# The down projection with seven products in every piece

## The chip, the cores and the metric

The kernel runs on one core of one Trainium2 chip. The metric is the time of one execution on the device in microseconds (us); smaller is better. All engines of the core work at once: TensorE (PE, with its weight loads as PEld), VectorE (DVE), ScalarE (ACT), GpSimd (POOL) and SyncE (SP). SP, ACT and POOL also issue DMAs, and each issues its own in the order of its queue.

## What is computed

One layer of a hybrid encoder on 512 tokens of width 2048, in float32. The part that matters here is the last one, the gated MLP with D_FF = 5504:

```
hn = rmsnorm(h, norm_ffn_g)
u = causal_dwconv(hn @ w_up, ffn_conv_w, ffn_conv_b)
gate, val = jnp.split(u, 2, axis=-1)
h = h + (jax.nn.silu(gate) * val) @ w_down
return rmsnorm(h, norm_out_g)
```

Before it come an mLSTM mixer and a short convolution (through `w_in`, `w_branch_m`, `w_branch_c`, `w_out`). The change touches the product with `w_down` (5504 x 2048) alone.

## The kernel before

**Products.** Every float32 operand is held as two rounded parts, hi and lo, and every product is three matmuls: hi by hi, hi by lo, lo by hi. Large products are made from pieces. A piece is a 2 x 2 block product: four blocks of weights (two output blocks, two pairs of the summed dimension) by blocks of activations of 256 tokens. By Strassen's scheme it takes 7 products, done for two halves r = 0, 1 of the summed dimension: 2 x 7 x 3 = 42 matmuls of 128 x 256. Done plainly it takes 8 products, 48 matmuls.

**A piece of seven products.** `weight_task` loads it into a `raw` buffer of seven slots (6 such buffers in all). A plain DMA on SP brings four blocks (L261). `fill` makes two sums while loading: SP copies a block into slots 4 and 5 (L251, L252), then POOL issues two DMAs that add a second block (L254). DVE makes the other two sums (L217, L222). ACT rounds each half to `wh` (L232, 4 buffers), DVE subtracts to get `wl` (L236, 3 buffers). **A piece of eight products** (`eight_task`) needs the four blocks alone: no L251, L252, L254, L217, L222; ACT has L185 and L186, DVE L190 and L191, twice each.

**Activations.** They are prepared two blocks at a time by a `cell_task`, which borrows a `raw` buffer as well. For seven products: the sums L343, L348, L353 on DVE, then 1792 columns in L357 (ACT) and L360 (DVE). For a pair that only pieces of eight products read: the difference L338, then 1536 columns in L357 and L360.

**Items.** An item is one pair of output blocks. Its pieces follow each other on PE; the first two items and the last two of a phase run piece by piece in turn. The down projection is three phases, here called chunks, of 8 items: chunk 1 has 4 pieces an item, chunks 2 and 3 have 3 (the last three blocks of the 5504 are done plainly at the end, in L1170 to L1172). Items are numbered 0 to 7 in a chunk. In the kernel before, the last piece of each item has eight products: 24 of the 80 pieces.

**After an item.** Six products gather in three PSUM banks of one of two sets, the seventh (P1) in bank 3, of which each set has one half. `evac_first` (L304, on ACT) copies P1 to a buffer `z`, and DVE adds the rest (L310 to L313). P1 of the next item is its first product in bank 3 and waits for that L304. There are three `z` buffers, used in turn, so item n + 3 takes the buffer of item n. The item's last act in the down projection is `down_post`: ACT changes a sign in `z` (L866), and POOL issues a DMA that adds `z` to `h_d` in DRAM (L156). L304 of item n + 3 has to wait until this DMA has landed.

**The order.** A loop over pieces (from L1303 on) writes the order of all engines by hand. In the turn of piece s it emits what DVE does for piece s + 1 (`wl`), the sums and `wh` for s + 2, cells that are due, the matmuls of s, `evac_first` if the item ends, and loads for as many buffers as are free by then. `down_post` is not tied to a turn. It waits in the list `posts` until a running account allows it:

```
                if not rush and cost and credit <= cost / 2 and len(x[1]) < due(x[0]) - s:
                    break
```

`credit` grows by 5.04 a piece and loses the costs that each task is given: 0.8 + 2.05 for a piece of seven, 0 + 1.5 for a piece of eight, 1.35 + 1.95 for a cell, 0.65 + 1.7 for a cell of eight, 2.3 for an evacuation. `due` is the last piece of item n + 3 in the down projection: one turn ahead of it, a post is let go whatever the account says. The order is fixed when the kernel is built.

Of the kernel before, what the change touches and what calls it, by code (L numbers as in the profile page):

```python
# [44 lines left out]
def kpair(c):  # L45

    q, r = divmod(c, 2)
    return 4 * q + r, 4 * q + 2 + r
# [23 lines left out]
def tile_block(ctx: ExitStack, tc: tile.TileContext, xT, w1, w_v0, w_v1, w_v2, w_bm, w_bc, w_out, w_up, w_down,  # L72
# [13 lines left out]
    def nm(s):  # L86
        uid[0] += 1
        return f"{s}_{uid[0]}"

    def f(ap):  # L90
        return ap.bitcast(F32)
# [4 lines left out]
    def slots(t):  # L96
        return t.rearrange("p (s n) -> p s n", n=SW)

    def two(ap):
        return ap.unsqueeze(1).to_broadcast([P, 2, ap.shape[-1]])  # L100
# [29 lines left out]
    def D_(shape, s):  # L130
        return dram.tile(shape, F32, name=s)
# [4 lines left out]
    a_d = D_([NF, P, T], "a_d")  # L136
# [16 lines left out]
    def add_to(dst, src, key):  # L153

        def fn():
            G.dma_start(dst, src, accum_op=ALU.add)  # L156
            stored.add(key)
        late.append(fn)

    def pair_ap(d, a, b):  # L160

        return d[a:b + 1:b - a].rearrange("j p t -> p j t")

    def sb_pair(t):
        return t[:, :2 * T].rearrange("p (j t) -> p j t", j=2)
# [79 lines left out]
    def fill(raw, srcs):  # L245

        def at(i):
            return raw[:, i * SW:(i + 1) * SW].rearrange("p (k n) -> p k n", n=P)

        a11, a12, a21, a22 = srcs  # L250
        SP.dma_start(at(4), a11)  # L251
        SP.dma_start(at(5), a22)  # L252
        for i in (4, 5):
            G.dma_start(at(i), a21, accum_op=ALU.add)  # L254

    def tiles_load(w, n1, n2, k0=0):
        def load(raw, q, bare=False):
            if not bare:
                fill(raw, [w[n, :, k0 + 4 * q + i:k0 + 4 * q + i + 2, :] for n in (n1, n2) for i in (0, 2)])
            src = w[n1:n2 + 1:n2 - n1, :, k0 + 4 * q:k0 + 4 * q + 4, :]  # L260
            SP.dma_start(raw[:, :4 * SW].rearrange("p (b m) -> p b m", b=2), src.rearrange("b p k n -> p b (k n)"))  # L261
        return load
# [53 lines left out]
    def cell_task(xs, c, d, scale=None, key=None, eight=False):  # L316

        k1, k2 = kpair(c) if isinstance(c, int) else c
        t = Task(None, None, None, None)

        def new_raw():
            t.raw = wp.tile([P, NW], F32, tag="raw", name=nm("xraw"), bufs=RAW)

        def load():
            new_raw()
            for dst, k in zip(t.two(), (k1, k2)):
                SP.dma_start(dst, d[k])

        def two_k():
            return (t.raw[:, :T], t.raw[:, T:2 * T]) if eight else (t.raw[:, 5 * SW:], t.raw[:, :2 * SW])  # L330

        def scaled():
            for ap, k in zip(two_k(), (k1, k2)):
                A.activation(ap, ap, AF.Copy, scale=scale(k))

        def diff():
            x = slots(t.raw)
            V.tensor_sub(x[:, 4:6], x[:, 0:4:2], x[:, 1:4:2])  # L338

        def t3():  # L340
            x = slots(t.raw)

            V.tensor_sub(x[:, 2:4], x[:, 1:6:4], two(x[:, 6]))  # L343

        def e():

            x = slots(t.raw)
            V.scalar_tensor_tensor(x[:, 4], x[:, 3], -1.0, x[:, 1], op0=ALU.mult, op1=ALU.subtract)  # L348

        def t4():  # L350

            x = slots(t.raw)
            V.scalar_tensor_tensor(x[:, 6], x[:, 4], -1.0, x[:, 0], op0=ALU.mult, op1=ALU.subtract)  # L353

        def hi():
            t.act = actp.tile([P, 2 * NW], F32R, tag="act", name=nm("act"))
            A.activation(t.act[:, :m], t.raw[:, :m], AF.Copy)  # L357

        def lo():
            V.tensor_sub(t.act[:, NW:NW + m], t.raw[:, :m], f(t.act[:, :m]))  # L360
            t.raw = None
            xs[t.cell] = t.act
            t.act = None

        t.load, t.sums, t.hi, t.lo, t.new_raw = load, [diff] if eight else [t3, e, t4], hi, lo, new_raw
        t.two, m = two_k, 6 * SW if eight else NW
        if scale:
            t.pre, t.behind = scaled, 1
        t.cost = (0.65, 1.7) if eight else (1.35, 1.95)
        t.ready = (lambda: all(k in stored for k in key)) if key else None  # L370
        return t
# [488 lines left out]
    def down_post(c, p):  # L860
        def post(it):
            j1, j2 = kpair(p)

            def fn():
                b = it.z[:, T:]
                A.activation(b, b, AF.Copy, scale=-1.0)  # L866
                add_to(pair_ap(h_d, j1, j2), sb_pair(it.z), ("d", c, p))
            return [(0.1, fn)]
        return post
# [24 lines left out]
    def phase(items, xs, cells, spread=(-4, -2, -1, 0, 2, 3, 5, 6)):  # L894

        inter = {0, len(items) - 2}
        e = len(steps)
        add(items, inter)
        for n, t in enumerate(cells):
            t.cell, t.xs, t.spread, t.after = n, xs, e + spread[n], 0  # L900
            if t.after_end:
                t.after_end.urgent = True
                t.after = [i for i in range(e) if steps[i][0] is t.after_end][-1] + 4
            use = [s for s in range(e, len(steps)) if steps[s][1] == n // 2]
            t.first, t.last = use[0], use[-1]
            all_cells.append(t)
# [86 lines left out]
    for c, (k0, nq) in enumerate(CHUNKS):  # L993
        AA = {}
        items = []
        for p in range(8):
            items.append(Item(tiles_load(w_down, *kpair(p), k0), nq, AA, down_post(c, p), None, nq - 1))
        cells = []
        for i in range(2 * nq):
            k1, k2 = (k0 + k for k in kpair(i))  # L1000
            cells.append(cell_task(AA, (k1, k2), a_d, None, [("a", k1), ("a", k2)], i >= 2 * nq - 2))
        phase(items, AA, cells)


# [237 lines left out]
    for i in range(at[START]):  # L1242
# [4 lines left out]
        while todo_mm:  # L1247
            s, r = todo_mm[0]
            it, q = steps[s]
            c = 2 * q + r  # L1250
# [245 lines left out]
```

## Time and profile before

| | |
|---|---|
| median of 3 runs | 2630.27 us (2627.07 to 2635.22) |
| profiled execution | 2635.24 us, its span 2633.5 us |
| PE busy, PEld busy | 2579.5 us, 2562.4 us |
| DVE, ACT, POOL busy | 2112.6, 1291.9, 799.5 us |
| matmuls | 21146, of them 20280 in L280 to L282 |
| mean granted TensorE clock | 0.990 |

The page is one execution: its span, and outside it 1.7 us. The tables by stretch give the microseconds that each engine was busy in a stretch and, in brackets, how many instructions it did. In rows of the timeline the first number is the start in us from the span's start, the second the time taken; idle time of the engine ahead of the row and what ended it stand in square brackets. On DVE an instruction's record overlaps that of the next a little, so what one costs in a row of others is the distance of the starts.

### The profile page before, as it was taken

The numbers are of one execution on the slowest core, as the hardware profiler recorded it, in microseconds if no ns is written. First come the engines' busy times: TensorE is split into PE (matmuls) and PEld (weight loads), VectorE is DVE, ScalarE is ACT, GpSimd is POOL, SyncE is SP. The second block draws the span as 40 slices with busy tenths as digits, with TensorE's granted clock in tenths as the row PEclk, the third lists the DMA queues.
The fourth block names the chain that finished last, engine by engine and source line by source line (L and its number), as shares of the span: only waits on it lengthen the run. The fifth ranks groups of instructions, "written<-read, shape, count | busy, mean of one in ns | idle before, by whom it ended". The sixth has DMA issues, their size and how long they took to land.

```text
span 2633.5 us, 55501 instructions
## 1 busy us (share of the span) xinstructions
PE 2579.5 (98%) x21146; PEld 2562.4 (97%) x21146; DVE 2112.6 (80%) x3308; ACT 1291.9 (49%) x1748; POOL 799.5 (30%) x922
## 2 busy tenths in 40 slices
PE   8999999999999999999899999999999999999997
PEld 8999999999999999999899999999999999999997
DVE  8577778886777888877989888888888897677756
ACT  7444554546556543435545544454444454444433
POOL 2443333333333211222333333333333323232310
PEclk8999999999999999999999999999999999999998
DMA  8799989898898897787898988988888889898976
GB/s 214 179 225 232 240 218 260 219 253 222 228 252 220 233 296 222 222 241 211 230 223 225 225 221 222 221 227 221 221 223 223 214 227 229 212 239 207 237 173 193
DMA packets 462557, 592.55 MB, mean 225 GB/s; under 512 B 42784, under 2 KB 296736, under 8 KB 462288
## 3 DMA queue, kind: packets, MB, share of 16 engines
q1 hardware_dynamic: 301968, 419.79, 50.8%
q0 software_dynamic: 133088, 124.04, 31.7%
q10 hardware_dynamic: 27232, 45.17, 4.7%
q8 instruction: 165, 2.70, 0.4%
q14 instruction: 104, 0.85, 0.1%
HBM read 531.17 MB, written 57.67 MB: 224 GB/s over the span
## 4 chain that ended last, share of the span: by engine, by line
PE 70%; DVE 4%; issue 1%; DMA 1%; ACT 0%; SPq 0%; DVEq 0%; POOL 0%; ACTq 0%; POOLq 0%
PE bank L282 22%; PE bank L280 22%; PE bank L281 22%; DVE wl L236 1%; DVE act L360 1%; DMA raw<-in_w_up_dram 1%; PE bank L1170 0%; PE bank L442 0%; PE bank L1171 0%; PE bank L1172 0%; PE bank L639 0%; DVE z L311 0%; DVE raw L217 0%; DVE z L310 0%; DVE xraw L343 0%
## 5 line engine op out<-in xcount | busy, mean ns | idle before, releaser
L280 PE MATMUL bank<-act,wh 128*128 128x256 f32 x6760 | 1929.3, 285 | 11.8 <-ACT wh L232 5.9
L282 PE MATMUL bank<-act,wl 128*128 128x256 f32 x6760 | 1920.5, 284 | 20.1 <-DVE wl L236 16.7
L281 PE MATMUL bank<-act,wh 128*128 128x256 f32 x6760 | 1917.9, 284 | 0.0
L282 PEld LDWEIGHTS bank<-act,wl 128*128 128x128 f32 x6760 | 1302.7, 193 | 24.0 <-DVE wl L236 19.9
L280 PEld LDWEIGHTS bank<-act,wh 128*128 128x128 f32 x6760 | 1302.8, 193 | 16.1 <-ACT wh L232 6.3
L232 ACT ACTIVATE wh<-raw 128x896 fp32r<-128x896 f32 x856 | 812.8, 953 | 1030.1 <-PE bank L281 700.6
L281 PEld LDWEIGHTS bank<-act,wh 128*128 128x128 f32 x6760 | 1302.9, 193 | 2.8 <-issue 1.7
L236 DVE TENSOR_TENSOR wl<-raw,wh 128x896 fp32r<-128x896 f32 x856 | 930.3, 1088 | 343.8 <-PE bank L282 232.9
L254 POOL DMA_DIRECT2D raw<-in_w_up_dram x344 | 298.9, 953 | 597.5 <-DMA raw<-in_w_up_dram 309.7
L254 POOL DMA_DIRECT2D raw<-in_w_dram x280 | 243.8, 945 | 519.2 <-DMA raw<-in_w_dram 338.3
L217 DVE TENSOR_TENSOR raw<-raw 128x256 f32<-128x256 f32 x428 | 179.9, 420 | 10.9 <-DMA raw<-in_w_down_dram 6.2
L254 POOL DMA_DIRECT2D raw<-in_w_down_dram x112 | 99.9, 1006 | 264.5 <-DMA raw<-in_w_down_dram 142.1
L222 DVE TENSOR_TENSOR raw<-raw 128x256 f32<-128x256 f32 x428 | 179.6, 420 | 0.3
L310 DVE TENSOR_TENSOR z<-bank,z 128x512 f32<-128x512 f32 x131 | 89.9, 687 | 34.7 <-ACT z L304 23.1
L357 ACT ACTIVATE act<-xraw 128x1792 fp32r<-128x1792 f32 (+1 forms) x52 | 85.6, 1647 | 55.8 <-DVE xraw L353 46.5
L185 ACT ACTIVATE wh<-raw 128x256 fp32r<-128x256 f32 x96 | 40.1, 417 | 136.9 <-PE bank L281 116.4
L360 DVE TENSOR_TENSOR act<-xraw,act 128x1792 fp32r<-128x1792 f32 (+1 forms) x52 | 101.8, 1958 | 0.0
L688 DVE TENSOR_TENSOR z<-z,rstd 128x1024 f32<-128x1024 f32 x83 | 101.1, 1219 | 0.2 <-ACT rstd L459 0.2
L190 DVE TENSOR_TENSOR wl<-raw,wh 128x256 fp32r<-128x256 f32 x96 | 40.5, 422 | 71.7 <-PE bank L282 41.2
L311 DVE TENSOR_TENSOR z<-bank,z 128x512 f32<-128x512 f32 x131 | 89.8, 686 | 1.7
L313 DVE TENSOR_TENSOR z<-bank,z 128x512 f32<-128x512 f32 x131 | 89.6, 684 | 0.0
L254 POOL DMA_DIRECT2D raw<-in_w_out_dram x48 | 41.8, 968 | 128.0 <-DMA raw<-in_w_out_dram 91.9
(214 smaller groups left out, 1389.5 us busy)
## 6 DMA issues: line engine op xcount, KB each, us to landing
raw<-in_w_up_dram SPq DMA_DIRECT2D x172, 512.0 KB, 5.6
raw<-in_w_dram SPq DMA_DIRECT2D x144, 512.0 KB, 5.9
raw<-in_w_up_dram SPq DMA_DIRECT2D x344, 128.0 KB, 4.0
raw<-in_w_up_dram POOLq DMA_DIRECT2D x344, 128.0 KB, 5.4
raw<-in_w_down_dram SPq DMA_DIRECT2D x80, 512.0 KB, 5.6
raw<-in_w_dram SPq DMA_DIRECT2D x280, 128.0 KB, 4.3
raw<-in_w_dram POOLq DMA_DIRECT2D x280, 128.0 KB, 5.3
raw<-in_w_out_dram SPq DMA_DIRECT2D x32, 512.0 KB, 4.8
```

The source lines that it names most:

```text
L217: V.tensor_add(x[:, 6], x[:, 5], x[:, 0])
L222: V.tensor_add(x[:, 2], x[:, 6], x[:, 1])
L232: A.activation(seven(t.wh[r]), half(r), AF.Copy)
L236: V.tensor_sub(seven(t.wl[r]), half(r), seven(f(t.wh[r])))
L254: G.dma_start(at(i), a21, accum_op=ALU.add)
L280: PE.matmul(ps, h, xh, start=start, stop=False, skip_group_check=True)
L281: PE.matmul(ps, h, xl, start=False, stop=False, skip_group_check=True)
L282: PE.matmul(ps, l, xh, start=False, stop=stop, skip_group_check=True)
L310: return [lambda: V.tensor_add(z[:, 0:4:3], b0, two(z[:, 1])), lambda: V.tensor_add(z[:, 1:3], b1, two(z[:, 3])), lambda: V.tensor_add(z[: ...
L311: lambda: V.tensor_add(z[:, 1:3], b1, two(z[:, 3])),
L360: V.tensor_sub(t.act[:, NW:NW + m], t.raw[:, :m], f(t.act[:, :m]))
L688: V.tensor_mul(sb_pair(it.z), sb_pair(it.z), two(rstd))
```

## The change

All pieces of the down projection become pieces of seven products, and all cells of it cells for seven. The down projection's items are no longer given `eight`, and its cells no longer the flag for it. The code that made pieces of eight stays, for the branch and output projections.

```
         for p in range(8):
-            items.append(Item(tiles_load(w_down, *kpair(p), k0), nq, AA, down_post(c, p), None, nq - 1))
+            items.append(Item(tiles_load(w_down, *kpair(p), k0), nq, AA, down_post(c, p)))
         cells = []
         for i in range(2 * nq):
             k1, k2 = (k0 + k for k in kpair(i))
-            cells.append(cell_task(AA, (k1, k2), a_d, None, [("a", k1), ("a", k2)], i >= 2 * nq - 2))
+            cells.append(cell_task(AA, (k1, k2), a_d, None, [("a", k1), ("a", k2)]))
         phase(items, AA, cells)
```

It also moves instructions, since the costs enter the account. Three places, by the program's order.

DVE at the start of chunk 1, from the second cell of its last pair to the end of the first changed piece (`xraw` and `act` belong to cells, `raw`, `wh`, `wl` to pieces; L848, L849, L688 and L855 are leftovers of the up projection). Before:

```order
L338 TENSOR_TENSOR xraw_2089_25826<-xraw_2089_25826 128x512
L360 TENSOR_TENSOR act_2088_25824<-xraw_2082_25766,act_2088_25824 128x1536
L848 SCALAR_TENSOR_TENSOR mA_88<-z1_93,pneg_72,mA_88 128x511
L849 SCALAR_TENSOR_TENSOR mA_88<-z1_93,pneg_72,mA_88 128x510
L688 TENSOR_TENSOR z0_92<-z0_92,rstd_79 128x1024
L190 TENSOR_TENSOR wl_2097_25901<-raw_2077_25711,wh_2092_25837 128x256
L191 SCALAR_TENSOR_TENSOR wl_2097_25901<-raw_2077_25711,wh_2092_25837 128x256
L190 TENSOR_TENSOR wl_2099_25907<-raw_2077_25711,wh_2094_25886 128x256
L191 SCALAR_TENSOR_TENSOR wl_2099_25907<-raw_2077_25711,wh_2094_25886 128x256
L360 TENSOR_TENSOR act_2095_25889<-xraw_2089_25826,act_2095_25889 128x1536
```

Now:

```order
L343 TENSOR_TENSOR xraw_2089_25836<-xraw_2089_25836 128x512
L360 TENSOR_TENSOR act_2088_25834<-xraw_2082_25770,act_2088_25834 128x1792
L348 SCALAR_TENSOR_TENSOR xraw_2089_25836<-xraw_2089_25836 128x256
L353 SCALAR_TENSOR_TENSOR xraw_2089_25836<-xraw_2089_25836 128x256
L848 SCALAR_TENSOR_TENSOR mA_88<-z1_93,pneg_72,mA_88 128x511
L849 SCALAR_TENSOR_TENSOR mA_88<-z1_93,pneg_72,mA_88 128x510
L688 TENSOR_TENSOR z0_92<-z0_92,rstd_79 128x1024
L217 TENSOR_TENSOR raw_2083_25773<-raw_2083_25773 128x256
L236 TENSOR_TENSOR wl_2097_25914<-raw_2077_25711,wh_2092_25849 128x896
L222 TENSOR_TENSOR raw_2083_25773<-raw_2083_25773 128x256
L236 TENSOR_TENSOR wl_2099_25919<-raw_2077_25711,wh_2094_25899 128x896
L360 TENSOR_TENSOR act_2095_25901<-xraw_2089_25836,act_2095_25901 128x1792
```

The same steps stand in the same order, with more and longer instructions in them; nothing is taken away on DVE.

ACT in chunk 1, around L304 of item 3, which reuses the buffer `z1` of item 0 (`raw_2123` is the first piece of item 4, `raw_2128` its second, `z0` and `z2` are the buffers of items 1 and 2). Before:

```order
L866 ACTIVATE z1_93<-z1_93 128x512
L866 ACTIVATE z0_92<-z0_92 128x512
L232 ACTIVATE wh_2145_26491<-raw_2123_26235 128x896
L232 ACTIVATE wh_2147_26540<-raw_2123_26235 128x896
L866 ACTIVATE z2_91<-z2_91 128x512
L232 ACTIVATE wh_2150_26553<-raw_2128_26296 128x896
L304 ACTIVATE z1_93<-bank3_83 128x256
```

Now:

```order
L232 ACTIVATE wh_2145_26488<-raw_2123_26239 128x896
L232 ACTIVATE wh_2147_26534<-raw_2123_26239 128x896
L866 ACTIVATE z1_93<-z1_93 128x512
L232 ACTIVATE wh_2150_26547<-raw_2128_26298 128x896
L304 ACTIVATE z1_93<-bank3_83 128x256
```

L866 of item 0 has moved from two turns ahead of that L304 to one, and L866 of items 1 and 2 have gone behind it (four and three turns later than before). It is let go at the last turn that `due` allows.

POOL at the start of chunk 2, around the adds of the last two items of chunk 1 (each row of L254 is one piece's two adding DMAs). Before:

```order
L254 DMA raw_2253_27732<-in_w_down_dram 128x256 x2
L254 DMA raw_2258_27793<-in_w_down_dram 128x256 x2
L156 DMA h_d_103<-z1_93 128x2x512
L156 DMA h_d_103<-z0_92 128x2x512
L254 DMA raw_2264_27857<-in_w_down_dram 128x256 x2
L254 DMA raw_2265_27863<-in_w_down_dram 128x256 x2
```

Now:

```order
L254 DMA raw_2253_27716<-in_w_down_dram 128x256 x2
L254 DMA raw_2258_27775<-in_w_down_dram 128x256 x2
L254 DMA raw_2259_27781<-in_w_down_dram 128x256 x2
L254 DMA raw_2264_27839<-in_w_down_dram 128x256 x2
L254 DMA raw_2265_27845<-in_w_down_dram 128x256 x2
L254 DMA raw_2270_27906<-in_w_down_dram 128x256 x2
L156 DMA h_d_103<-z1_93 128x2x512
L156 DMA h_d_103<-z0_92 128x2x512
```

The adds of `z1` and `z0` now stand behind the fills of four more pieces, the first of which and the fourth were pieces of eight and had no L254 before. On ACT their L866 are let go one turn ahead of the L304 that reuses `z1`, where before there were three turns. At the start of chunk 3 the same happens to the last two items of chunk 2: the add of item 6 is let go one turn ahead of its buffer's reuse by item 1 (three before), that of item 7 one turn ahead of its reuse by item 2 (six before). Item 1 of chunk 1 is let go two turns ahead (six before).

More of the change, by code (lines that the diff above doesn't have):

```diff
@@ L996, in tile_block @@
         for p in range(8):
-            items.append(Item(tiles_load(w_down, *kpair(p), k0), nq, AA, down_post(c, p), None, nq - 1))
+            items.append(Item(tiles_load(w_down, *kpair(p), k0), nq, AA, down_post(c, p)))
         cells = []
@@ L1000, in tile_block @@
             k1, k2 = (k0 + k for k in kpair(i))
-            cells.append(cell_task(AA, (k1, k2), a_d, None, [("a", k1), ("a", k2)], i >= 2 * nq - 2))
+            cells.append(cell_task(AA, (k1, k2), a_d, None, [("a", k1), ("a", k2)]))
         phase(items, AA, cells)
```

## The prediction

> **What bounds the kernel now.** I read the head of the page, then the busy times by stretch (one of the up projection, then the down projection cut at the starts of its chunks), then who PE waits for in the down projection.
>
> ```profile
> span 2633.5 us, 55501 instructions
> ...
> core 0: us, PE busy (x) PEld busy (x) DVE busy (x) ACT busy (x) POOL busy (x), PEclk, DMA share, GB/s
> 1340.00:2100.00 760.00, 760.00 (x6336) 760.00 (x6335) 672.87 (x986) 374.93 (x458) 261.80 (x302) 1.00 0.89 223
> ...
> 2139.60:2185.10 45.50, 42.55 (x351) 41.94 (x350) 45.03 (x65) 23.57 (x32) 10.50 (x12) 1.00 0.91 249
> 2185.10:2311.60 126.50, 125.46 (x1046) 125.26 (x1045) 88.82 (x144) 56.24 (x80) 38.96 (x42) 1.00 0.88 213
> 2311.60:2344.40 32.80, 31.99 (x267) 31.79 (x266) 26.37 (x40) 14.91 (x22) 9.52 (x10) 1.00 0.89 230
> 2344.40:2439.40 95.00, 95.00 (x794) 95.00 (x793) 65.79 (x109) 42.62 (x64) 28.55 (x30) 1.00 0.91 218
> 2439.40:2472.70 33.30, 31.93 (x266) 31.73 (x265) 26.92 (x40) 14.87 (x22) 8.60 (x9) 1.00 0.91 234
> 2472.70:2567.70 95.00, 95.00 (x794) 95.00 (x793) 56.16 (x92) 37.85 (x62) 23.61 (x24) 1.00 0.82 194
> ...
> PE bank L282 <- DVE wl L236: 5.0, 4, 1.6
> PE bank L280 <- ACT z L304: 1.0, 1, 1.0
> ```
>
> PE sets the time: in the up projection, whose pieces all have seven products, it is never idle, and 6336 matmuls in 760 us make 0.120 us each. In the down projection it waits 6.0 us in all, and only at the starts of the three chunks (in the stretches of 45.5, 32.8 and 33.3 us, and early in the next one); there cells are made as well, and in the first stretch DVE is busy 45.03 of 45.5 us.
>
> **Removed on PE.** 24 pieces lose 6 matmuls each: 144 x 0.120 = 17.3 us, all on the path.
>
> **Added on DVE.** The rows are from the start of chunk 1.
>
> ```profile
> 2149.58 0.68 DVE L343 TENSOR_TENSOR xraw<-xraw 128x512 f32<-128x512 f32 x1
> ...
> 2151.10 0.42 DVE L217 TENSOR_TENSOR raw<-raw 128x256 f32<-128x256 f32 x1
> 2151.43 1.08 DVE L236 TENSOR_TENSOR wl<-raw,wh 128x896 fp32r<-128x896 f32 x1
> 2152.44 0.42 DVE L222 TENSOR_TENSOR raw<-raw 128x256 f32<-128x256 f32 x1
> ...
> 2154.38 2.02 DVE L360 TENSOR_TENSOR act<-xraw,act 128x1792 fp32r<-128x1792 f32 x1
> 2156.31 0.42 DVE L348 SCALAR_TENSOR_TENSOR xraw<-xraw 128x256 f32<-128x256 f32 x1
> ...
> 2167.28 0.69 DVE L338 TENSOR_TENSOR xraw<-xraw 128x512 f32<-128x512 f32 x1
> 2167.88 1.75 DVE L360 TENSOR_TENSOR act<-xraw,act 128x1536 fp32r<-128x1536 f32 x1
> 2169.55 0.75 DVE L848 SCALAR_TENSOR_TENSOR mA<-z,pneg,mA 128x511 f32<-128x511 f32 x1
> ...
> 2172.13 0.42 DVE L190 TENSOR_TENSOR wl<-raw,wh 128x256 fp32r<-128x256 f32 x1
> ...
> 2172.80 0.42 DVE L190 TENSOR_TENSOR wl<-raw,wh 128x256 fp32r<-128x256 f32 x1
> ...
> 2188.41 0.69 DVE L310 TENSOR_TENSOR z<-bank,z 128x512 f32<-128x512 f32 x1 [0.49 <-ACT z L304]
> ...
> 2188.43 0.39 PE L280 MATMUL bank<-act,wh 128*128 128x256 f32 x1 [1.04 <-ACT z L304]
> ...
> 2164.00:2188.40 24.40, 23.39 (x195) 23.19 (x194) 23.49 (x36) 12.86 (x22) 8.73 (x10) 1.00 0.98 270
> ```
>
> From start to start: L217 0.33, L222 0.33, L236 1.01, so a piece of seven costs 2.68; a piece of eight has two pairs at 0.67 (2172.13 to 2172.80), 1.34. Each changed piece adds 1.34. A cell of seven has its three sums in 1.52 (2149.58 to 2151.10) and L360 in 1.93, a cell of eight 0.60 and 1.67: each of the six changed cells adds 1.18. Amid the chunks DVE has room (24 x 1.34 = 32 us against, in the three long stretches alone, some 106 idle), so there I cost it at nothing; without that room it would be up to 1.34 a piece. ACT's added 0.24 us a piece (two L232 for four shorter ones) lies beside PE everywhere, at nothing too.
>
> At the start of chunk 1 there is no room: from 2164 to 2188.4 DVE is busy 23.49 of 24.40 us, and PE's wait at 2188.43 ends with L304, which by the program's order stands on ACT behind a store of what DVE makes as its last leftover of the up projection. Two pieces and two cells come in ahead of it: 2 x 1.34 + 2 x 1.18 = 5.0, less some 0.3 of DVE's idle time. PE gets there 4.7 later instead of 1.4 (12 matmuls) earlier: 6.1 us against the saving. At the starts of chunks 2 and 3 the two changed pieces before them add 2.7, of which DVE's waits for PE just before hide most; 0.6 reaches PE's wait for `wl` there instead of 1.4 gained, and the next two cells some 0.3 more: 2.3 each. DVE's terms: 6.1 + 2.3 + 2.3 = 10.7; bounds 5 (the leftovers give way) and 13 (nothing hidden).
>
> **The posts.** This is where the account moves work. The rows are ACT's and POOL's around L304 of item 3 of chunk 1, the landing times of L156, and ACT's and POOL's at the start of the last piece of item 1 of chunk 2.
>
> ```profile
> 2218.03 1.14 ACT L866 ACTIVATE z<-z 128x512 f32<-128x512 f32 x2
> ...
> 2222.50 0.96 ACT L232 ACTIVATE wh<-raw 128x896 fp32r<-128x896 f32 x1 [1.57 <-PE bank L281]
> 2223.36 0.61 ACT L866 ACTIVATE z<-z 128x512 f32<-128x512 f32 x1
> ...
> 2228.86 0.39 ACT L304 ACTIVATE z<-bank 128x256 f32<-128x256 f32 x1 [2.54 <-DMA h_d<-z]
> ...
> 2219.89 3.15 POOL L156 DMA_DIRECT2D h_d<-z  x2
> ...
> 2228.05 0.87 POOL L254 DMA_DIRECT2D raw<-in_w_down_dram  x1 [1.47 <-DMA raw<-in_w_down_dram]
> 2228.61 1.56 POOL L156 DMA_DIRECT2D h_d<-z  x1
> ...
> DMA to landing us min/median/max: 6.0/9.3/14.3
> ...
> 2338.76 0.96 ACT L232 ACTIVATE wh<-raw 128x896 fp32r<-128x896 f32 x1 [1.67 <-PE bank L281]
> ...
> 2342.77 0.86 POOL L254 DMA_DIRECT2D raw<-in_w_down_dram  x1 [0.81 <-DMA raw<-in_w_down_dram]
> ```
>
> The last piece of item 3 starts at about 2222.4 (PE has just released the L232). The add of item 0 was issued at 2219.89; L304 has waited for its landing and runs at 2228.86. PE needs bank 3 after 48 + 18 matmuls, at 2222.4 + 7.9 = 2230.3, so nothing is lost, by 1.4 us. In the changed kernel that add takes the place that the single L866 at 2223.36 and L156 at 2228.61 have now (item 2's), behind the same piece's L254, which waits for its own load. Issued 6.2 after the start of the piece and landed 9.3 later, it lets L304 finish 15.9 after it; PE, with 42 + 18 matmuls, is there after 7.2. That is a wait of 8.7. POOL is some 2 us freer there, since the pair at 2219.89 has gone: I take 6.5. Bounds: 3.2 (issue at 4.0, as soon as L866 and POOL's L254 can be through, landing in 6.0) and 13.7 (landing in 14.3).
>
> Item 1's add, two turns ahead, is let go 5.04 earlier but behind three pieces' L254: 2.3 (0 to 6). Items 6 of chunk 1 and of chunk 2 (reused by item 1 of the next chunk) stand behind two more fills still on their way: at 2342.77, 4.0 after the start of that piece (2338.76), POOL only reached the last but one of them. With one more (1 to 4 us) and 0.9 for it the add is issued after 5.9 to 8.9, and 9.3 + 0.4 - 7.2 on top make 8.4 to 11.4: 9.5 and, with one add there for two, 9.0 (4 to 16 each). Item 7 of chunk 2 is like the first, with two adds together: 7.5. Sum 6.5 + 2.3 + 9.5 + 9.0 + 7.5 = 34.8.
>
> **The clock.** After waits of 2.2 and 1.9 us the granted clock halved:
>
> ```profile
> 1261.12 0.58 PE L282 MATMUL bank<-act,wl 128*128 128x256 f32 x1 [1.89 <-DVE wl L236]
> ...
> 1261.50:1267.00 5.50, 5.50 (x27) 5.50 (x27) 5.50 (x9) 0.87 (x2) 1.44 (x2) 0.50 0.75 180
> ```
>
> 27 matmuls in 5.5 us lose 27 x (0.204 - 0.120) = 2.3. The four long waits are longer than these, so I add 4 x 2.1 = 8.5, a little less because `wl` for the next piece is late as well (0 to 11). The Trainium skill (TensorE: Matmul & The Clock Gate, the part on the HAM clock gate) says that one idle window of about 3.4 us halves the clock and one busy window restores it; by that each long wait costs 1.7 and the forecast would be 2 us less. The row shows a longer half-clock stretch, and I keep the row.
>
> **Sum.** -17.3 + 10.7 + 34.8 + 8.5 = +36.7. Against the profiled execution's 2635.24 (span 2633.5 and 1.7 around it) that is 2672; it ran 5.0 above the median 2630.27, so I forecast 2667 as a median.
>
> **Rivals.**
> - *PE alone counts: faster.* DVE's additions and the late adds are hidden, 17.3 us are gained: 2613. For it: PE has no idle time in 2344 to 2439, and the up projection runs nothing but pieces of seven. Against it: L304 waiting for the landing at 2228.86 with 1.4 us to spare, and the add now 8 us later. It decides for this rival if the add has landed 6.8 us after the start of the piece; with an issue at 4.0 that leaves 2.8 us for a landing, and the shortest of 24 is 6.0. The Trainium skill (Perfetto Trace Analysis, Identifying the Most-Contended Engine) would have the engine of highest occupancy cut first, for TensorE by its weight loads; PEld is busy 95.00 of 95.00 us in two of the long stretches, and by that rule alone this rival is the forecast. Chance 0.04.
> - *The gain is eaten at the chunk starts, and the adds land in time: no change.* -17.3 + 10.7 = -6.6: 2624. It needs the same of all five adds, while DVE is as I have it; that the adds are shorter in an emptier queue speaks for it, the 6.0 of the shortest against it. Chance 0.06.
> - *DMA becomes the bound: slower, but less.* Rows:
>
> ```profile
> q1 hardware_dynamic: 301968, 419.79, 50.8%
> q0 software_dynamic: 133088, 124.04, 31.7%
> ...
> 1250.00:1256.00 6.00, 6.00 (x52) 6.00 (x51) 3.36 (x4) 3.59 (x4) 1.72 (x2) 1.00 1.04 298
> ```
>
> A changed piece loads 0.26 MB more through each queue; at their time per byte (0.508 x 2633.5 / 419.79 and 0.317 x 2633.5 / 124.04) that is 0.84 + 1.76 = 2.6 us of all 16 engines. From 2344 to 2439 the six changed pieces bring the 0.91 x 95 = 86.5 to 102 against 90.7 of PE. If a share of 1.0 were the limit, the long stretches would lose some 12, 5 and 3 us against PE alone: -17.3 + 10.7 + 20 = +13, 2644. Against it: a share of 1.04 is reached at 1250, and the waits above give DMA 35 us more. Chance 0.08.
>
> **How the numbers follow.** The forecast has 0.80, its own range 2645 to 2690; 0.02 is left for a still longer time. Low end: DVE 5, waits at their floors 3.2 + 0 + 4 + 4 + 3.2, clock 5: +7, 2637; raised to 2642, since all floors together are unlikely. High end: DVE 12, waits 53 (each about 11, the second 5), clock 11: +59, 2689. So 2641 to 2689, which also takes in the DMA case. A difference under 0.3% (7.9 us) is about what these measurements can't tell from no change: faster 0.04, same 0.07, slower 0.89.
>
> **What would show it.** Matmuls in L280 to L282 fall by 144. Idle time of PE by ACT z L304 (1.0 us here) becomes the largest PE wait, about 35 us, in four places: 0.1 to 0.2 of an item into item 4 of chunk 1, item 2 of chunks 2 and 3, item 3 of chunk 3; ahead of each, L304 on ACT waits for h_d<-z by 6 to 10 us, and the clock shows halves behind it. L310 at the start of chunk 1 comes some 4.7 us later. It is wrong if L304 no longer waits for h_d<-z, if the landings shrink to 6 us in the emptier queue, or if PE's new waits are for `wl` or loads instead.

## The result, and the profile after

The changed kernel takes 2666.5 us (median of 4 runs, 2663.46 to 2668.12), the kernel before in the same comparison 2632.7 (4 runs). The ratio on record is 1.0139, 95% interval 1.0124 to 1.0155; the two medians alone give 1.0128. The forecast was 2667. In later comparisons of 18 to 29 runs each the kernel before has medians of 2627.5, 2629.2 and 2627.5.

The page's head and three of its groups (instruction, tiles, count, busy us, mean ns, idle time ahead and what ended most of it), then who PE waits for in the down projection (us in total, times, longest):

```profile
span 2665.3 us, 55407 instructions
PE 2568.8 (96%) x21002; PEld 2549.0 (96%) x21002; DVE 2147.3 (81%) x3320; ACT 1303.0 (49%) x1700; POOL 839.0 (31%) x970
...
L280 PE MATMUL bank<-act,wh 128*128 128x256 f32 x6712 | 1918.5, 286 | 46.9 <-ACT z L304 37.5
L282 PE MATMUL bank<-act,wl 128*128 128x256 f32 x6712 | 1909.3, 284 | 28.3 <-DVE wl L236 24.5
...
L304 ACT ACTIVATE z<-bank 128x256 f32<-128x256 f32 x131 | 48.1, 367 | 66.0 <-DMA h_d<-z 51.1
```

```profile
PE bank L280 <- ACT z L304: 37.5, 6, 10.1
PE bank L282 <- DVE wl L236: 11.7, 8, 2.1
```

PE has 144 matmuls less and is busy 10.7 us less, yet the span is longer: PE waits 37.5 us for L304, which was 1.0 before, and L304 itself waits 51.1 us for the adds into `h_d`. The same stretches as in the prediction, cut at the starts of this execution's pieces:

```profile
core 0: us, PE busy (x) PEld busy (x) DVE busy (x) ACT busy (x) POOL busy (x), PEclk, DMA share, GB/s
2134.80:2182.30 47.50, 41.60 (x339) 40.59 (x338) 47.11 (x65) 24.03 (x27) 15.80 (x19) 1.00 0.95 252
2182.30:2319.20 136.90, 124.69 (x1010) 123.88 (x1009) 97.25 (x144) 58.98 (x69) 45.98 (x50) 0.96 0.92 219
2319.20:2353.00 33.80, 31.02 (x254) 30.41 (x253) 31.22 (x45) 16.58 (x19) 12.98 (x16) 1.00 0.98 256
2353.00:2454.90 101.90, 92.67 (x759) 92.46 (x758) 73.05 (x110) 44.72 (x52) 39.41 (x43) 0.95 1.00 237
2454.90:2488.70 33.80, 31.02 (x255) 30.41 (x254) 30.68 (x44) 16.00 (x18) 13.31 (x16) 1.00 0.97 251
2488.70:2600.30 111.60, 94.30 (x758) 93.89 (x757) 65.79 (x97) 41.25 (x52) 33.86 (x36) 0.92 0.85 197
```

The two long stretches that PE filled in 95.00 us now take 101.9 and 111.6, with idle time and a clock under 1.00. One of the five places, item 2 of chunk 2: ACT's and POOL's rows in the stretch before PE's wait, PE's first matmul after it, and the clock in the wait, behind it, and later.

```profile
2348.97 1.14 ACT L866 ACTIVATE z<-z 128x512 f32<-128x512 f32 x2
...
2364.13 0.38 ACT L304 ACTIVATE z<-bank 128x256 f32<-128x256 f32 x1 [12.55 <-DMA h_d<-z]
...
2352.20 1.75 POOL L254 DMA_DIRECT2D raw<-in_w_down_dram  x2 [2.43 <-DMA raw<-in_w_down_dram]
2355.54 1.75 POOL L254 DMA_DIRECT2D raw<-in_w_down_dram  x2 [1.59 <-DMA raw<-in_w_down_dram]
2356.61 3.15 POOL L156 DMA_DIRECT2D h_d<-z  x2
...
2364.56 0.58 PE L280 MATMUL bank<-act,wh 128*128 128x256 f32 x1 [9.23 <-ACT z L304]
...
2358.10:2364.50 6.40, 0.00 (x0) 0.00 (x0) 0.00 (x0) 0.37 (x2) 3.49 (x4) 0.50 1.14 217
2364.60:2368.40 3.80, 3.80 (x18) 3.80 (x19) 3.77 (x7) 1.70 (x2) 0.00 (x0) 0.50 0.72 119
2368.40:2380.00 11.60, 11.60 (x98) 11.60 (x98) 8.32 (x13) 5.71 (x8) 4.33 (x6) 1.00 0.70 169
```

L866 starts at 2349.0 and is done at 2350.1, but L156 starts at 2356.6, 7.6 after the start of L866: POOL stands at two pieces' fills (L254), each of which waits for its own load. By the record of its DMA the first add has landed at 2364.05, 7.4 after its issue; L304, and behind it PE, go on at once. Of the half clock, 6.4 us lie inside the wait and cost nothing; the 3.8 us behind it cost 3.80 - 18 x 0.120 = 1.6.

**Where the time is.** The profiled executions reach the down projection 2130.1 to 2139.6 us after their start, though up to 2000 us the order of PE's, DVE's, ACT's and POOL's instructions is the same in all. So I compare the down projection alone: PE's matmuls are counted off piece by piece in each trace, and the table has the microseconds from start to start (the sums are of the unrounded numbers). The kernels below the first two are explained in the next section.

| | chunk 1, first 12 pieces | its rest | chunk 2, first 6 | its rest | chunk 3, first 6 | its rest | sum |
|---|---|---|---|---|---|---|---|
| before | 67.6 | 104.4 | 32.7 | 95.0 | 33.3 | 94.9 | 428.1 |
| after | 71.9 | 112.6 | 33.8 | 101.9 | 33.8 | 111.6 | 465.4 |
| more_buffers | 73.0 | 100.8 | 33.8 | 90.7 | 33.8 | 90.6 | 422.7 |
| account_of_before | 71.5 | 102.2 | 33.8 | 94.3 | 33.8 | 92.6 | 428.2 |
| posts_at_once | 71.5 | 100.8 | 35.6 | 90.9 | 37.2 | 90.6 | 426.6 |
| late_posts_alone | 67.6 | 113.1 | 32.5 | 96.2 | 33.6 | 97.2 | 440.2 |
| no_fills_amid | 74.3 | 103.6 | 33.8 | 92.0 | 34.2 | 93.0 | 431.0 |
| chunk1_eight | 67.7 | 104.4 | 31.7 | 90.7 | 33.8 | 90.6 | 418.9 |
| copy_first | 71.7 | 100.8 | 33.8 | 90.7 | 33.8 | 90.6 | 421.4 |
| store_last | 71.0 | 100.8 | 33.8 | 90.7 | 33.8 | 90.6 | 420.7 |
| before_five_buffers | 67.6 | 104.4 | 32.5 | 95.0 | 33.4 | 94.9 | 427.9 |
| eight_in_chunk1_store_last | 67.3 | 104.4 | 31.8 | 91.0 | 33.8 | 90.6 | 418.9 |

### The profile page after: what moved, and what is told of

The parts are those of the page before. It is cut to its first block, busy times and chain, and to the rows that moved or that the text cites. A ratio compares the mean times of both kernels' runs of the same rounds, so it can differ in the third digit from the quotient of the medians.

```text
span 2665.3 us, 55407 instructions
## 1 busy us (share of the span) xinstructions
PE 2568.8 (96%) x21002; PEld 2549.0 (96%) x21002; DVE 2147.3 (81%) x3320; ACT 1303.0 (49%) x1700; POOL 839.0 (31%) x970
## 4 chain that ended last, share of the span: by engine, by line
PE 75%; DVE 6%; DMA 4%; issue 2%; ACT 0%; POOL 0%; SPq 0%; DVEq 0%; POOLq 0%; ACTq 0%
PE bank L280 24%; PE bank L282 24%; PE bank L281 24%; DMA h_d<-z 2%; DVE act L360 1%; DVE wl L236 1%; DMA raw<-in_w_down_dram 1%; PE bank L639 1%; PE bank L442 0%; PE bank L1170 0%; DMA xraw<-a_d 0%; DMA raw<-in_w_up_dram 0%; DVE xraw L343 0%; DVE raw L217 0%; PE bank L1171 0%
## 5 line engine op out<-in xcount | busy, mean ns | idle before, releaser
L280 PE MATMUL bank<-act,wh 128*128 128x256 f32 x6712 | 1918.5, 286 | 46.9 <-ACT z L304 37.5
L232 ACT ACTIVATE wh<-raw 128x896 fp32r<-128x896 f32 x904 | 857.0, 952 | 1062.5 <-PE bank L281 724.6
L236 DVE TENSOR_TENSOR wl<-raw,wh 128x896 fp32r<-128x896 f32 x904 | 981.3, 1087 | 352.0 <-PE bank L282 236.1
L254 POOL DMA_DIRECT2D raw<-in_w_up_dram x344 | 299.0, 961 | 598.4 <-DMA raw<-in_w_up_dram 329.4
L254 POOL DMA_DIRECT2D raw<-in_w_dram x280 | 243.8, 955 | 512.7 <-DMA raw<-in_w_dram 328.2
L254 POOL DMA_DIRECT2D raw<-in_w_down_dram x160 | 144.7, 1030 | 284.4 <-DMA raw<-in_w_down_dram 186.0
L217 DVE TENSOR_TENSOR raw<-raw 128x256 f32<-128x256 f32 x452 | 189.5, 419 | 10.5 <-DMA raw<-in_w_down_dram 5.2
L222 DVE TENSOR_TENSOR raw<-raw 128x256 f32<-128x256 f32 x452 | 189.0, 418 | 0.3
L310 DVE TENSOR_TENSOR z<-bank,z 128x512 f32<-128x512 f32 x131 | 89.7, 685 | 69.1 <-ACT z L304 66.9
L688 DVE TENSOR_TENSOR z<-z,rstd 128x1024 f32<-128x1024 f32 x83 | 101.0, 1217 | 0.2 <-ACT rstd L459 0.2
L254 POOL DMA_DIRECT2D raw<-in_w_out_dram x48 | 41.8, 967 | 127.9 <-DMA raw<-in_w_out_dram 91.4
L304 ACT ACTIVATE z<-bank 128x256 f32<-128x256 f32 x131 | 48.1, 367 | 66.0 <-DMA h_d<-z 51.1
L312 DVE TENSOR_TENSOR z<-bank,z 128x256 f32<-128x256 f32 x131 | 55.6, 424 | 4.5
```

Of the source, the lines that this page charges most:

```text
L217: V.tensor_add(x[:, 6], x[:, 5], x[:, 0])
L222: V.tensor_add(x[:, 2], x[:, 6], x[:, 1])
L232: A.activation(seven(t.wh[r]), half(r), AF.Copy)
L236: V.tensor_sub(seven(t.wl[r]), half(r), seven(f(t.wh[r])))
L280: PE.matmul(ps, h, xh, start=start, stop=False, skip_group_check=True)
L310: return [lambda: V.tensor_add(z[:, 0:4:3], b0, two(z[:, 1])), lambda: V.tensor_add(z[:, 1:3], b1, two(z[:, 3])), lambda: V.tensor_add(z[: ...
```

## The experiments

The theory is the prediction's: the account lets the adds go too late, and L304 pays for it. Rivals: DMA is the bound, or the longer work on DVE is.

**account_of_before: the account of before, the pieces of after.**

```
+            if i >= 2 * nq - 2:
+                cells[-1].cost = (0.65, 1.7)
...
+    for (it, q), t in zip(steps, wt):
+        if isinstance(it, Item) and it.num > 106 and q == it.nq - 1:
+            t.cost = (0, 1.5)
```

> Seven products everywhere as in the changed kernel, but the account is charged as before (0 + 1.5 for the last piece of an item, 0.65 + 1.7 for the last two cells of a chunk), so that every L866, L156 and L304 stands in the turn that it has in the kernel before. Late posts as the cause: the waits of PE for ACT z L304 (37.5 us) and the half clock behind them go; what is left is -17.3 for the matmuls and +10.7 for DVE at the chunk starts, -6.6 against before, about 2626 (2622 to 2632; the add of item 0 has two turns, and one more fill of POOL ahead of it may cost up to 3). Rival, DMA as the bound: the 2.6 us of all 16 engines that each of the 24 pieces adds are not touched, and the time stays above the kernel before, about 2644. Rival, the longer sums and cells themselves: it stays near 2666.

Measured: 2629.6 against 2627.5, ratio 1.0008 (0.9999 to 1.0017). Within the theory's range (2622 to 2632), but towards its upper end. PE's waits for L304 fall from 37.5 to 7.1; 2.5 of these are DVE's doing, at the start of chunk 1. Two and three turns ahead of L304, where the posts stood before, is not quite early enough any more:

```profile
2328.14 1.13 ACT L866 ACTIVATE z<-z 128x512 f32<-128x512 f32 x2
...
2332.10 1.75 POOL L254 DMA_DIRECT2D raw<-in_w_down_dram  x2 [1.58 <-DVE wl L236]
2333.18 3.15 POOL L156 DMA_DIRECT2D h_d<-z  x2
...
2345.13 0.39 PE L280 MATMUL bank<-act,wh 128*128 128x256 f32 x1 [1.84 <-ACT z L304]
```

L156 comes 3.9 us after the end of L866, behind the fills, and PE waits 1.84 for the L304 behind it. Three such waits, with the clock behind one of them, make the rests of the chunks 1.4, 3.6 and 2.0 longer than in more_buffers: 7.0 of the 12.2 us that the matmuls bring there.

**more_buffers: the order of after, z in five buffers.**

```
+                if it.num >= 107:
+                    it.z = (zs[1], zs[0], z2, mB[:, :2 * T], mA[:, :2 * T])[(it.num - 107) % 5]
-    lbufs = (mA, mB, zs[0], zs[1])
+    lbufs = (mA, zs[1], zs[0], z2)
```

(`it.num` 107 is the first item of the down projection; `lbufs` are the buffers of the squares in the last norm, which follows it, in a new order because `mB` is now a `z`.)

> The changed kernel with its own order of ACT and POOL, instruction for instruction, but the down projection's z goes round five buffers (mA and mB, free by then, beside the three), so that L304 waits for the add of the item five before it and not three. Late posts as the cause: it is the reuse of the buffer that costs, so PE's waits for L304 fall from 37.5 to about 2 (the one at the start of chunk 1, which is DVE's, stays) and the time to about 2626 (2621 to 2632), though not one post is let go earlier. Rival, the order itself (L866 and L156 in the way of wh or of the fills): no better than 2650. Rival, DMA as the bound: about 2644.

Measured: 2621.85, ratio 0.9977 (0.9966 to 0.9987); the down projection takes 5.4 us less than before. ACT and POOL do the same work in the same order as in the changed kernel, and 43 us of the down projection are gone. PE's waits, and most of the rest of chunk 2:

```profile
PE bank L282 <- DVE wl L236: 11.4, 8, 2.0
PE bank L280 <- ACT z L304: 2.5, 1, 2.5
...
2337.80:2426.90 89.10, 89.10 (x745) 89.10 (x744) 69.83 (x104) 42.58 (x49) 38.09 (x40) 1.00 1.08 263
```

The one wait for L304 that is left is DVE's, at the start of chunk 1. Amid the chunk PE is busy for all of 89.1 us while the DMA share stands at 1.08: the share is the time of packets over 16 engines and no limit at 1.0. That ends the rival of a DMA bound. So it is neither the late issue as such nor the traffic that costs, but that z is used again before the add has landed.

**late_posts_alone: the pieces of before, the account of after.**

```
+            cells[-1].cost = (1.35, 1.95)
...
+    for (it, q), t in zip(steps, wt):
+        if isinstance(it, Item) and it.num > 106:
+            t.cost = (0.8, 2.05)
```

> The kernel before, with its pieces and cells of eight products, but the account charged as if all were of seven (0.8 + 2.05 a piece, 1.35 + 1.95 a cell): every L866, L156 and L304 stands in the turn that it has in the changed kernel. Late posts as the cause: waits of PE for L304 in the same five places, each 0.7 shorter by the six more matmuls ahead of P1 and up to 2 shorter since the pieces of eight leave POOL's queue emptier; 15 to 32 us in all, with the half clock 5 to 8 more: 2653 to 2670, about 2660. Rival, the loads that the pieces of seven add make the adds late: without them the waits stay under 8 us, and the time under 2645.

Measured: 2641.9, ratio 1.0053 (1.0038 to 1.0067). My expectation missed: the waits at the five places are 5.9, 0, 1.1, 1.4 and 0.7, in all 9.1, little above the rival's 8, and the time lies under the rival's 2645 and below my range of 2653 to 2670. The same place as above, item 2 of chunk 2:

```profile
2345.68 1.14 ACT L866 ACTIVATE z<-z 128x512 f32<-128x512 f32 x2
...
2353.22 0.38 ACT L304 ACTIVATE z<-bank 128x256 f32<-128x256 f32 x1 [4.57 <-DMA h_d<-z]
...
2346.59 2.55 POOL L156 DMA_DIRECT2D h_d<-z  x2
```

L156 starts 0.9 us after L866 here, against 7.6 in the changed kernel, since POOL is through with its fills. Late posts alone cost 12 us here, against 43 in the changed kernel; the rest needs the fills of the added pieces as well.

**no_fills_amid: the changed kernel without the fills where the adds stand.** Items 2 to 5 of each chunk are loaded without fills, and DVE makes their two sums.

```
+    def bare(it, q):
+        return (it.num, q) in ALONE or it.num >= 107 and (it.num - 107) % 8 in (2, 3, 4, 5)
```

> The changed kernel with its three buffers and its order of L866, L156 and L304; the pieces of items 2 to 5 of each chunk are loaded without L251, L252 and L254 (DVE makes those two sums as well, one more instruction a piece, where it has room). So POOL's queue is free of fills where the five late adds stand. If it is the fills that hold L156 back (3.3 to 8.0 us from L866 to L156 in the changed kernel), L156 follows L866 by about 1 us, lands 6 to 8 later, and the waits fall from 35.8 to about 9 (0 to 2.5 each), with 2 for the clock: about 2632 (2626 to 2640). If it is the landing itself or the late L866, the waits stay above 25 and the time above 2650. If DVE has no room for the sums, PE waits for wl amid the chunks.

Measured: 2636.0, ratio 1.0025 (1.0014 to 1.0035), within the range of 2626 to 2640 that I gave. The lines of the code stand 3 lower here (L869 and L307 are L866 and L304):

```profile
2346.16 1.14 ACT L869 ACTIVATE z<-z 128x512 f32<-128x512 f32 x2
...
2352.94 0.38 ACT L307 ACTIVATE z<-bank 128x256 f32<-128x256 f32 x1 [4.18 <-DMA h_d<-z]
...
2347.07 2.45 POOL L156 DMA_DIRECT2D h_d<-z  x2 [15.27 <-ACT z L869]
```

L156 starts 0.9 after L866 and lands in 5.8 us instead of 7.4. The five waits are 1.3, 0.9, 1.0, 0.9 and 1.0: 5.1 in place of 35.8, and none of them halves the clock. The posts are as late as in the changed kernel. This shows that the fills are the other half of the cause. The edit takes away POOL's issues and their traffic together; of 8.4 gained here (from the wait of 9.4 to 1.0) the earlier issue in POOL's queue has 6.7 and the shorter landing 1.6. The down projection is 8.3 us longer than in more_buffers, the median 14; where the other 6 lie stays open.

**posts_at_once: no cost for a down post.** `return [(0.1, fn)]` in `down_post` becomes `return [(0, fn)]`.

> The changed kernel, with the cost of a down post set to 0, so that the account never holds one back: L866 and L156 are issued in the turn that ends with the evacuation, 6 turns or more ahead of the L304 that reuses the buffer (1 and 2 in the changed kernel). Late posts as the cause: no wait for an add anywhere, -17.3 + 10.7, about 2626; if L866 or L156 at the chunk starts are in the way of wh or the fills, up to 5 more: 2621 to 2631. Rival, DMA as the bound: about 2644, with PE waiting for wl, wh or raw amid the chunks.

Measured: 2630.1, ratio 1.0005 (0.9997 to 1.0014). No add is late, yet it is 8.3 us slower than more_buffers by the medians; the down projections of the two profiled executions account for 3.9 of that, and for 5.4 at the same clock (see the last section); the rest stays open. DVE and POOL late in the start of chunk 2:

```profile
2336.89 0.43 DVE L217 TENSOR_TENSOR raw<-raw 128x256 f32<-128x256 f32 x1 [3.78 <-DMA raw<-in_w_down_dram]
...
2324.30 1.93 POOL L156 DMA_DIRECT2D h_d<-z  x1
...
2336.06 0.86 POOL L254 DMA_DIRECT2D raw<-in_w_down_dram  x1 [4.20 <-DMA raw<-in_w_down_dram]
```

At the chunk starts loads are late instead: POOL's fill waits 4.2 us for its load, DVE 3.8 for the fill, and PE for `wl` (15.6 us in 11 waits, 11.4 in 8 with five buffers). The starts of chunks 2 and 3 take 35.6 and 37.2 in place of 33.8. That the early adds are what makes these loads late was not tried by itself.

**chunk1_eight: five buffers, pieces of eight in chunk 1 alone.**

```
+            items.append(Item(tiles_load(w_down, *kpair(p), k0), nq, AA, down_post(c, p), None, None if c else nq - 1))
...
+            cells.append(cell_task(AA, (k1, k2), a_d, None, [("a", k1), ("a", k2)], c == 0 and i >= 2 * nq - 2))
```

> Five buffers as in more_buffers, but in chunk 1 the last piece of each item has eight products again, and its last two cells are cells of eight; chunks 2 and 3 have seven throughout. It prices DVE at the start of chunk 1. If seven products there cost DVE what the stages of more_buffers say (7.5 with the half clock behind it, against the 5.8 that 48 matmuls bring), chunk 1 goes back from 173.8 to 172.0 as before, chunks 2 and 3 stay at 33.8 + 90.6, and the time is some 2 us below more_buffers: about 2620 (2616 to 2624). If DVE's part at the chunk start is not the price (it is noise of one profile, or the chunk would pay it with pieces of eight too), chunk 1 takes 5 or more us longer than in more_buffers: 2627.

Measured: 2619.3, ratio 0.9964 (0.995 to 0.9978). The first 12 pieces of chunk 1 take 67.7 in place of 73.0, the rest 104.4 in place of 100.8: seven products lose 5.3 at this start (3.8 where the clock stays full, as in account_of_before) and gain 3.6 in all the rest of the chunk. Chunk 2 gains another 2.1 at its start, which I had not expected; two changed pieces less stand ahead of it, but that this is the reason was not tried. The interval of this run overlaps that of more_buffers, so the difference between the two is read from the stages and not from the times.

**copy_first and store_last: L304 ahead of the store.** Both with five buffers. copy_first puts the stores that a turn holds (`dmas`) behind `evac_first`; store_last puts there the store of a leftover that `flush` releases in the same turn.

```
 copy_first:
+        swap = main and it.num >= 107 and q == it.nq - 1
+        if not swap:
+            for fn in dmas:
+                fn()
...
             evac_first(it)
+            if swap:
+                for fn in dmas:
+                    fn()

 store_last:
-            flush_late()
+            if upto < 104:
+                flush_late()
...
             evac_first(it)
+            if it.num > 106:
+                flush_late()
```

> Five buffers as in more_buffers; at the end of an item of the down projection ACT does L304 ahead of the stores (L149) of that turn instead of behind them. In more_buffers ACT stood 4.7 us at the store of the last leftover of the up projection, which waits for DVE's L855, and PE waited 2.7 for the L304 behind it, with 1.5 of half clock after that. If that place is on the path, both go and the time falls by up to 4.2: about 2618 (2616 to 2621). Rival: DVE is the bound there anyway, wl of the next piece is late instead (DVE was idle for 0.5 us only), and no more than 1 us is gained: 2621 (2620 to 2624).

> Five buffers and seven products everywhere as in more_buffers; the one store of the last leftover of the up projection that stands ahead of L304 in ACT's queue at the start of chunk 1 (L149, a_d from mB) now stands behind it. copy_first did not move it: both stood there because the leftover is flushed between the two. If that queue is what PE waits for, the wait of 2.7 for ACT z L304 goes, and with it the half clock that follows it in some runs: chunk 1 falls from 173.8 (172.3 at full clock) to 169.7, the time from 2622 to about 2619. Rival: DVE is the bound and only 0.5 us idle there; then wl of the next piece comes late instead, and less than 1 us is gained.

copy_first moved nothing: in ACT's rows the store still stands ahead of L304. So it is more_buffers once more: 2623.2, 0.9977 (0.9968 to 0.9987). store_last moved it: 2622.1, 0.9976 (0.9963 to 0.9988). ACT in copy_first, then ACT and PE in store_last:

```profile
2184.09 0.33 ACTq L149 DMA_DIRECT2D a_d<-mB  x1
2184.46 0.38 ACT L304 ACTIVATE z<-bank 128x256 f32<-128x256 f32 x1 [4.68 <-DVE raw L217]
...
2178.38 0.36 ACT L304 ACTIVATE z<-bank 128x256 f32<-128x256 f32 x1
2182.78 0.33 ACTq L149 DMA_DIRECT2D a_d<-mB  x1
...
2186.13 0.39 PE L282 MATMUL bank<-act,wl 128*128 128x256 f32 x1 [1.87 <-DVE wl L236]
```

L304 comes 4.9 us earlier in its chunk (the executions are 1.2 apart at its start), and PE then waits 1.9 for `wl` where it waited 2.5 for L304: 0.6 us are gained. The rival holds: L304, behind ACT's queue, is what PE's wait is put down to, but DVE is what is late.

**before_five_buffers: a control.** The kernel before with `z` in five buffers, by the same edit as in more_buffers.

> A control: the kernel before, with its pieces of eight, and z in five buffers as in more_buffers. In the kernel before PE waits for L304 once, 1.0 us, and that one is DVE's at the start of chunk 1, so five buffers should bring nothing: the same time as before within 0.1%, the down projection 428 us. Rival: the buffers help by themselves, and the gain of more_buffers (5.7) is theirs and not the matmuls': then 3 us or more faster than before.

Measured: 2627.3, ratio 0.9999 (0.9989 to 1.0008). The gain of more_buffers is that of the matmuls.

**eight_in_chunk1_store_last: the lowest median.** The edits of chunk1_eight and of store_last together.

> A candidate for the best: chunk1_eight (five buffers, pieces of eight in chunk 1 alone) with that store behind L304. The wait of 1.2 us for L304 at the start of chunk 1 goes if the store is what it stands behind: down projection 417.7 us instead of 418.9, time 2618 (2615 to 2621), some 10 below before. If wl takes its place: 2619 as chunk1_eight.

Measured: 2616.7, ratio 0.9956 (0.9944 to 0.9969), 10.8 us below before and some 50 below the changed kernel. My 2618 assumed that the wait of 1.2 us goes; it does, but a wait for `wl` takes half of it back. Its interval overlaps that of chunk1_eight, and the down projection takes 418.9 in both: the store's place is worth nothing that can be told here.

## Why the prediction was right, point by point

- **Matmuls, -17.3:** 6712 x 3 against 20280 is 144 less, as counted.
- **DVE, +10.7:** right in the sum. Against before, the stretch of 12 pieces at the start of chunk 1 is 4.2 longer though 18 matmuls (2.2) are gone: 6.4 (6.1 predicted). The prediction let all of it reach PE at L304; PE meets it earlier too, in new waits of 2.3 and 1.4 us for `wl` and 0.8 for `act`, and waits 2.6 instead of 1.2 for L304 (from the starts of its matmuls, less their step). The starts of chunks 2 and 3 are 1.0 and 0.5 longer with 12 less: 2.5 and 1.9 (2.3 each). Amid the chunks DVE's additions cost nothing: the rest of chunk 2 with five buffers takes 90.7 us, and 18 pieces of 42 matmuls at 0.120 are 90.7. L310 stands 53.75 after the start of the chunk against 48.81: 4.9 later (4.7).
- **Late adds, +34.8:** from the starts of PE's matmuls, less their step of 0.12, the five waits are 6.5, 2.4, 9.4, 10.3 and 7.3, in all 35.8 (6.5, 2.3, 9.5, 9.0, 7.5). The parts inside were each a little off and made up for one another: in the long waits L156 was issued up to 8.9 us after the start of the piece, at the end of my range, and landed in 7.4 to 8.7 instead of 9.3, with a median of 8.6 over all 24. L304 itself waited 9.6 to 12.9 us for its add in the four places where the prediction looked for 6 to 10.
- **The clock, +8.5:** the sum was near and its parts were wrong. I gave 2.1 to each of four waits and nothing to the fifth, of 2.4 us. In the 8 us behind the five waits PE did 55, 55, 52, 53 and 54 matmuls of 66.7: 1.4, 1.4, 1.8, 1.6 and 1.5, in all 7.7. The estimate of 1.7 for each long wait, worked out from the window of some 3.4 us in the Trainium skill (TensorE: Matmul & The Clock Gate, the part on the HAM clock gate), was nearer here than the row that I kept instead, whose stretch of 5.5 us stood behind two waits in a row. As the least idle time that halves the clock that window doesn't hold: the wait of 2.4 us did it too, and so did one of 2.0 in account_of_before (16 matmuls in the 3 us behind it, where 25 fit).
- **The sum:** +36.7 predicted, +37.4 measured in the down projection. That the median met the forecast to 1 us has luck in it: the executions vary by more, and the kernel before's median was 2632.7 in that comparison and 2627.5 to 2629.2 later. Three slips in the working change nothing here: the low end was worked out as 2642 and written as 2641, the high end took 12 for DVE where its bound was 13, and the 1.4 us that PE had to spare at 2230.3 were 1.0, since L304 ends 0.39 after its start.
- **The rivals:** PE alone counts (2613) and no change (2624) both need the adds in time. With the adds out of the way (more_buffers) the time is 2621.9, 5.6 below before: the second of them, with its -6.6, is near to what the change is worth by itself. The DMA bound (2644) is refuted by the share of 1.08 beside a PE that never waits.

What the prediction didn't say is how the cause divides. It took late posts and fills together; either alone is far cheaper (in the down projection, late posts with pieces of eight cost 12 us against before, late posts without fills amid the chunks 8 against more_buffers, both together 43 against more_buffers).

## What to carry to other kernels

When a change takes work off the bounding engine, look first at what the order's planner does with the new costs: here a saving of 17 us became a loss of 37 because an account put a DMA behind other work, one turn ahead of the reuse of its buffer. Ask of each buffer in turn what the last reader is, in which queue it stands, and how many turns lie between; two more buffers made the order harmless without moving an instruction. And price a change by stage: with five buffers the same change won 4.3 us in the long stretch of each later chunk, and in chunk 1 lost at the start what the rest gained; the versions that leave it out there have the lowest medians.

## What the runs showed of the hardware

- Of two waits of the same length one can halve the clock and the other not. The same wait for L304 at the start of chunk 1, in more_buffers and then in copy_first, each with 3 us that begin 1.4 after its end:

```profile
2183.98 0.39 PE L280 MATMUL bank<-act,wh 128*128 128x256 f32 x1 [2.45 <-ACT z L304]
...
2185.40:2188.40 3.00, 3.00 (x17) 3.00 (x16) 2.96 (x5) 1.89 (x4) 1.30 (x2) 0.53 0.82 198
...
2184.89 0.39 PE L280 MATMUL bank<-act,wh 128*128 128x256 f32 x1 [2.45 <-ACT z L304]
...
2186.30:2189.30 3.00, 3.00 (x27) 3.00 (x26) 2.97 (x5) 2.59 (x4) 1.67 (x2) 1.00 0.64 140
```

  17 matmuls against 27 after waits of the same 2.45 us; in the 8 us behind the wait PE does 54 against 66, so it costs 1.5 us or nothing. The Trainium skill (TensorE: Matmul & The Clock Gate, the part on the HAM clock gate) says that the gate looks at a free-running window, so that the phase decides; these two executions agree with that. Of PE's waits for L304 amid the chunks, in all runs and from the starts of its matmuls, the five of 5.9 us or more halved it, and so did those of 2.0 and 2.4; those of 1.8 us and less did not.
- Executions differ where the code does not. From PE's first piece to the ninth it takes 57.6 us in more_buffers and 62.3 in the profiled execution of before, whose instructions there are the same and in the same order:

```profile
0.00:100.00 100.00, 88.91 (x647) 85.72 (x648) 72.63 (x109) 59.81 (x79) 29.31 (x51) 0.91 0.76 193
...
0.00:100.00 100.00, 89.28 (x680) 85.71 (x681) 75.61 (x113) 60.61 (x79) 31.72 (x53) 0.97 0.80 202
```

  The first row is before, with a clock of 0.91, the second more_buffers with 0.97. Of the twelve executions nine take 57.6 to 59.0 us there, and the three with pieces of eight in every chunk (before, late_posts_alone, before_five_buffers) 61.7 to 62.5; why is open. From the ninth piece to the down projection another 7.8 us lie between the shortest (2059.6) and the longest (2067.4). A difference of 5 us between two kernels is told by the stage that was changed, not by two spans.
